# Query heads of the sliding attention transposed in pairs

## The chip, the cores and the metric
The kernel runs on one core of one Trainium2 chip. The metric is the device time of one execution in microseconds (us), lower is better. The engines are TensorE (PE for its matmuls, PEld for its weight loads), VectorE (DVE), ScalarE (ACT), GpSimd (POOL) and SyncE (SP), which issues the DMAs. Each works through its own queue of instructions in order; semaphores hold an instruction until what it needs is there.

## The reference
A decoder trunk of two layers on 1024 tokens of width 1024, float32. Three mixers read one normalised projection of 1312 columns; their outputs are concatenated, projected and added, and a gated feed-forward follows. The change touches the first mixer, sliding-window attention with 6 query heads on 2 key-value heads of 64, cut here to what matters:

```python
q = rms_norm(q.reshape(B, S, SWA_HEADS, HEAD_DIM), q_gain)
k = rms_norm(k.reshape(B, S, SWA_KV_HEADS, HEAD_DIM), k_gain)
s = jnp.einsum('bnqhgd,bnkhd->bnhgqk', qb, kb).astype(jnp.float32) * (HEAD_DIM ** -0.5)
s = jnp.where(mask[None, :, None, None], s + bias[None, None], -jnp.inf)
lse = jnp.logaddexp(jax.nn.logsumexp(s, axis=-1, keepdims=True), sk)
o = jnp.einsum('bnhgqk,bnkhd->bnqhgd', jnp.exp(s - lse).astype(v.dtype), vb)
```

Each block of 128 queries sees its own 128 keys and the 128 before.

## The kernel before
Each layer is three functions. `phase1` (from L283) goes over 8 tiles of 128 tokens: normalise and transpose the input tile (`head`, L330), project it in three pieces of 512, 512 and 288 columns (`proj`, L377, lines 381 to 383), and from these compute the sliding attention, the pooling mixer and the inputs of the latent attention. `phase2` (L545) is the latent attention with the output projection w_out (L787 to L817 and L795 to L797); `phase34` is the feed-forward.

Products are made of pieces: an operand is split into a high part, rounded to the type float32r by ACT, and a low part, the rest, by DVE (`split`, L57), and a product adds the piece products that matter. For the scores (L513, L514) the trick is in the contraction of 128: one operand holds the high part of a query head on partitions 0 to 63 and its low part on 64 to 127, and the key stands in both halves, so that one matmul adds both.

To get there, a tile's projected queries and keys `qk` (8 heads of 64: six of queries, two of keys) are multiplied by their norms into `dup`, in two rounds of four heads, each head written twice side by side (L401). Four PE transposes per round (L406) put 128 columns, one head in both halves, into one bank of PSUM, `tq`. ACT writes the scaled high part over all 128 partitions (L409), DVE overwrites the lower half with the low part (L410); the second round has two query heads and the two key heads, whose parts go to `kr5` by `split` (L414). `dup` is one buffer; `tq` shares a one-bank pool, `ps_ta`, with the transposes of L447 and L459 (in tile 7, `ps_th` with those of L339).

```python
tp = (ps_th if t >= 7 else ps_ta).tile([P, 4, P], F32, name="tq", tag="th" if t >= 7 else "ta")
sc.activation(dst, tp[:, 0:nq], AF.Copy, scale=gqc)
```

The program is written tile by tile; a scheduler sets the order on each engine across the tiles from its own estimates of durations, and pools decide what waits for a buffer. So an edit in one place can move instructions all over phase 1.

Of the kernel before, what the change touches and what calls it, by code (L numbers as in the profile page):

```python
# [11 lines left out]
F32 = mybir.dt.float32  # L12
# [3 lines left out]
AF = mybir.ActivationFunctionType  # L16
ALU = mybir.AluOpType
# [4 lines left out]
P = 128  # L22
# [14 lines left out]
def trunk(ctx: ExitStack, tc: tile.TileContext, A, out):  # L37
# [65 lines left out]
    for l in range(DEPTH):  # L103
        xsrc = A["x"][0] if l == 0 else xres
        G = dict(
            ident=ident, xm=xm, xrow=xrow, krr=krr, rc=rc, cosT=cosT, sinT=sinT, sinks=sinks,
            pscale=pscale, invc=invc, nhalf=nhalf, gq=gq, gm=gm, cmask=cmask, identr=identr, rn=rn, gc=gc, g32=g32, xsrc=xsrc, dram=dram, gap=gap, xp=xp, gns=ExitStack(), bias_keep=bias_keep)
        phase1(nc, tc, A, l, pool, split, f, bcast, G, (gq, gk, gmk, dram) if l == 0 else None)
        phase2(nc, tc, A, l, pool, split, f, bcast, G)
        phase34(nc, tc, A, l, pool, split, f, bcast, G, xres, out)  # L110


def rstd_of(nc, ms, n, nhalf):
    nc.gpsimd.tensor_scalar(out=ms, in0=ms, scalar1=EPS, scalar2=None, op0=ALU.add)
    nc.gpsimd.tensor_tensor(out=ms, in0=ms, in1=nhalf[:, 0:n], op=ALU.pow)
    return ms
# [16 lines left out]
def tables(nc, tc, load, A, bcast, early, one, evq, ps, kr5, G, more):  # L133
    ve, sc, gp, te, sy = nc.vector, nc.scalar, nc.gpsimd, nc.tensor, nc.sync
# [5 lines left out]
    sy.dma_start(rel[0:32], A["rel_bias"])  # L140
    hot = evq.tile([P, 512], F32, name="hot", tag="qk")[:, 0:384]
    sy.dma_start(hot[0:33], A["hot"])
    flip = evq.tile([P, 4, 128], F32, name="flip", tag="dup")
    sy.dma_start(flip[:, 0], A["flip"])
    acc = ps.tile([P, 512], F32, name="po")
    te.matmul(acc[0:6, 0:384], rel[0:33], hot[0:33], start=True, stop=True)
# [9 lines left out]
    for i in range(3):  # L156
        acc = ps.tile([P, 512], F32, name="po")
        c = slice(512 * i, 512 * i + 512)
# [65 lines left out]
    def cut(v, bits):  # L224
# [6 lines left out]
        out=ang, in0=posf.unsqueeze(2).to_broadcast(shp),  # L231
        in1=ifr.unsqueeze(1).to_broadcast(shp), op=ALU.mult,
# [33 lines left out]
    def wrap(v):  # L266
        up, dn = tmp(), tmp()
        ve.tensor_scalar(out=up, in0=v, scalar1=float(np.pi), scalar2=None, op0=ALU.is_gt)
        ve.tensor_scalar(out=dn, in0=v, scalar1=-float(np.pi), scalar2=None, op0=ALU.is_lt)
        fma(up, -TWO_PI, v, v)  # L270
        fma(dn, TWO_PI, v, v)
        ve.tensor_scalar(out=up, in0=v, scalar1=LIM, scalar2=-LIM, op0=ALU.min, op1=ALU.max)
        return up
# [5 lines left out]
    c = wrap(rs)  # L279
# [3 lines left out]
def phase1(nc, tc, A, l, pool, split, f, bcast, G, setup):  # L283
    ve, sc, gp, te, sy = nc.vector, nc.scalar, nc.gpsimd, nc.tensor, nc.sync
    cosT, sinT = G["cosT"], G["sinT"]
    ident, xm, xrow, krr = G["ident"], G["xm"], G["xrow"], G["krr"]
    with ExitStack() as ph:
# [9 lines left out]
        evq = pool(ph, f"p1q_{l}")  # L297
# [11 lines left out]
        ps_th = pool(ph, f"p1th_{l}", bufs=1, space=PSUM)  # L309
        ps_ta = pool(ph, f"p1ta_{l}", bufs=1, space=PSUM)  # L310
# [44 lines left out]
        kr5 = one.tile([P, 2, 2, 3 * P], F32R, name="kr5")  # L355
        if l == 0:
            tables(nc, tc, load, A, bcast, early, ev, evq, ps_o, kr5, G, setup)
# [3 lines left out]
        for g in range(4):  # L361
            o = 64 * (g % 2)
# [8 lines left out]
        for t in range(NT):  # L371
# [17 lines left out]
            qk = evq.tile([P, 512], F32, name="qk")  # L389
# [5 lines left out]
            r8 = rstd_of(nc, ms8, 8, G["nhalf"])  # L395
            qs = two.tile([P, 6, P], F32R, name="qs")
            gqc = G["gq"][:, l : l + 1]
            for b in range(2):
                dup = evq.tile([P, 4, 2, 64], F32, name="dup")
                sh = [P, 4, 2, 64]  # L400
                ve.tensor_tensor(  # L401
                    out=dup, in0=qk[:, 256 * b : 256 * b + 256].rearrange("p (h d) -> p h d", h=4).unsqueeze(2).to_broadcast(sh),
                    in1=r8[:, 4 * b : 4 * b + 4].unsqueeze(2).unsqueeze(3).to_broadcast(sh), op=ALU.mult)
                tp = (ps_th if t >= 7 else ps_ta).tile([P, 4, P], F32, name="tq", tag="th" if t >= 7 else "ta")
                for j in range(4):
                    te.transpose(tp[:, j], dup[:, j].rearrange("p a c -> p (a c)"), ident)  # L406
                nq = 4 if b == 0 else 2
                dst = qs[:, 4 * b : 4 * b + nq]
                sc.activation(dst, tp[:, 0:nq], AF.Copy, scale=gqc)  # L409
                ve.scalar_tensor_tensor(  # L410
                    out=dst[64:128], in0=tp[64:128, 0:nq], scalar=gqc[64:128], in1=f(dst[64:128]),
                    op0=ALU.mult, op1=ALU.subtract)
            kc = slice(slot * P, slot * P + P)
            split(kr5[:, 0, :, kc], kr5[:, 1, :, kc], tp[:, 2:4])  # L414
            if slot == 2:
                gp.tensor_copy(kr5[:, :, :, 0:P], f(kr5[:, :, :, 2 * P : 3 * P]))

# [28 lines left out]
            tp = ps_ta.tile([P, 4, P], F32, name="ta")  # L446
# [11 lines left out]
            tp = ps_ta.tile([P, 4, P], F32, name="ta")  # L458
# [4 lines left out]
            if t % 2 == 1:  # L463
                W = 16 + 2 * P
                for k in range(2):
# [4 lines left out]
                    if k == 1:  # L470
# [5 lines left out]
                                     in1=sa[64:128, st - hs : W - hs], op=ALU.add)  # L476
                    dd = one.tile([P, 2 * P], F32, name="dd")
                    for g, src in ((2 * k, sa), (2 * k + 1, sb)):
# [4 lines left out]
                            out=dd[pr], in0=src[pr, 16:W], scalar=wv, in1=u[pr, 16:W],  # L483
# [21 lines left out]
            for g in range(2):  # L505
# [3 lines left out]
                for i0, ni in ((0, 2), (2, 1)):  # L509
                    s = ps_sc.tile([P, 2, 256], F32, name="s")  # L510
                    for i in range(i0, i0 + ni):
                        h = 3 * g + i
# [4 lines left out]
                                     in1=G["bias"][:, h0 : h0 + ni, 256 - nk : 256], op=ALU.add)  # L517
                ve.tensor_reduce(mx[:, gs], Pt[:, :, 0 : nk + 1], AX.X, ALU.max, negate=True)
                for i in range(3):
                    h = 3 * g + i  # L520
# [3 lines left out]
                for i in range(3):  # L524
                    h = 3 * g + i
# [3 lines left out]
                for b in range(nb):  # L529
                    tp = ps_tp.tile([P, 4, P], F32, name="tp")  # L530
                    for i in range(3):
# [9 lines left out]
                                 in1=ob[0:64].rearrange("p (a b) -> p a b", a=3), op=ALU.add)  # L541
# [757 lines left out]
```

## Time and profile before

| | |
|---|---|
| three runs | 2209.97, 2216.93, 2217.36 us, median 2216.93 |
| profiled execution | 2210.4 us, its span 2208.6 us |
| granted TensorE clock, mean | 0.985 of full speed |
| PE busy | 2114.1 us, 96% |
| DVE busy | 1692.3 us, 77% |
| ACT busy | 1087.7 us, 49% |
| POOL busy | 976.2 us, 44% |

Phase 1 of layer 0 runs from the start to about 200 us, that of layer 1 from about 1109 to 1290 us; each overlaps the beginning of phase 2. The span begins at zero; a share of busy time is an average over the span, and a matmul's busy time runs from its start to a modelled end, while the next one may have started.

### The profile page before, as it was taken

The numbers are of one execution on the slowest core, as the hardware profiler recorded it, in microseconds if no ns is written. First come the engines' busy times: TensorE is split into PE (matmuls) and PEld (weight loads), VectorE is DVE, ScalarE is ACT, GpSimd is POOL, SyncE is SP. The second block draws the span as 40 slices with busy tenths as digits, with TensorE's granted clock in tenths as the row PEclk, the third lists the DMA queues.
The fourth block names the chain that finished last, engine by engine and source line by source line (L and its number), as shares of the span: only waits on it lengthen the run. The fifth ranks groups of instructions, "written<-read, shape, count | busy, mean of one in ns | idle before, by whom it ended". The sixth has DMA issues, their size and how long they took to land.

```text
span 2208.6 us, 29772 instructions
## 1 busy us (share of the span) xinstructions
PE 2114.1 (96%) x10468; PEld 1766.5 (80%) x10468; DVE 1692.3 (77%) x2595; ACT 1087.7 (49%) x2300; POOL 976.2 (44%) x916
## 2 busy tenths in 40 slices
PE   7998999999999999999989988999999999999999
PEld 5887788877788888788868867988778888887887
DVE  5567888898988787765845678887998888877657
ACT  5778767563434333311257786665634343343111
POOL 1433647245544452532614344462465444425215
PEclk8999999999999999999999999999999999999999
DMA  7002221323534435975530022113234443359754
GB/s 220 1 1 80 82 77 39 106 96 133 181 134 166 149 125 198 412 296 188 200 113 1 1 95 77 68 49 102 96 144 165 144 171 134 142 217 412 278 200 162
DMA packets 137932, 312.16 MB, mean 141 GB/s; under 512 B 17297, under 2 KB 68152, under 8 KB 137784
## 3 DMA queue, kind: packets, MB, share of 16 engines
q1 hardware_dynamic: 137784, 310.27, 39.4%
q8 instruction: 83, 1.36, 0.3%
q14 instruction: 65, 0.53, 0.1%
HBM read 203.53 MB, written 106.70 MB: 140 GB/s over the span
## 4 chain that ended last, share of the span: by engine, by line
PE 70%; DVE 10%; DMA 8%; ACT 6%; POOL 3%; issue 2%; SPq 1%; ACTq 0%; POOLq 0%; DVEq 0%
PE gu L1149 10%; PE gu L1147 10%; PE gu L1148 10%; PE dn L994 5%; PE dn L996 5%; PE dn L995 5%; PE acc L381 3%; PE acc L382 3%; PE acc L383 3%; DMA rw<-in_w_down_dram 2%; PE tp L756 2%; DMA raw<-in_w_in_dram 1%; PE ss L732 1%; PE po L766 1%; DMA raw<-in_w_gate_dram 1%
## 5 line engine op out<-in xcount | busy, mean ns | idle before, releaser
L1149 PE MATMUL gu<-T,sb 128*128 128x512 f32 x704 | 274.8, 391 | 9.8 <-DVE sb L58 9.7
L1147 PE MATMUL gu<-T,sb 128*128 128x512 f32 x704 | 274.9, 390 | 4.6 <-ACT sb L58 2.5
L1148 PE MATMUL gu<-T,sb 128*128 128x512 f32 x704 | 274.0, 389 | 0.0
L994 PE MATMUL dn<-op,ga 128*128 128x512 f32 x616 | 241.3, 393 | 7.4 <-DMA ga<-gd 7.4
L995 PE MATMUL dn<-op,ga 128*128 128x512 f32 x616 | 241.4, 392 | 0.0
L996 PE MATMUL dn<-op,ga 128*128 128x512 f32 x616 | 240.6, 392 | 0.0
L58 ACT CAST go<-xm 128x512 fp32r<-128x512 f32 x154 | 95.1, 620 | 274.4 <-POOL xm L1181 94.2
L943 POOL TENSOR_TENSOR rw<-rw 128x1536 f32<-128x1536 f32 (+1 forms) x32 | 112.4, 3522 | 257.0 <-DVE op L953 163.5
L1124 POOL TENSOR_TENSOR xm<-raw 128x512 f32<-128x512 f32 x44 | 68.6, 1561 | 319.9 <-DMA raw<-in_w_up_dram 122.8
L952 ACT CAST op<-rw 128x1536 fp32r<-128x1536 f32 (+1 forms) x56 | 76.9, 1376 | 266.7 <-PE dn L996 253.8
L58 DVE TENSOR_TENSOR go<-xm,go 128x512 fp32r<-128x512 f32 x154 | 154.4, 1012 | 34.1 <-ACT go L58 30.1
L58 ACT CAST sb<-raw 128x512 fp32r<-128x512 f32 x180 | 110.4, 617 | 122.5 <-PE gu L1149 99.6
L1149 PEld LDWEIGHTS gu<-T,sb 128*128 128x128 f32 x704 | 132.1, 188 | 41.3 <-DVE sb L58 13.9
L1147 PEld LDWEIGHTS gu<-T,sb 128*128 128x128 f32 x704 | 132.2, 188 | 34.5 <-ACT sb L58 4.6
L1181 POOL TENSOR_TENSOR xm<-xm 128x512 f32<-128x512 f32 x88 | 143.3, 1637 | 30.4 <-DVE go L58 19.6
L1148 PEld LDWEIGHTS gu<-T,sb 128*128 128x128 f32 x704 | 132.2, 188 | 27.4
L58 DVE TENSOR_TENSOR sb<-raw,sb 128x512 fp32r<-128x512 f32 x180 | 152.9, 850 | 1.0
L953 DVE TENSOR_TENSOR op<-rw,op 128x1536 fp32r<-128x1536 f32 (+1 forms) x56 | 113.8, 2032 | 40.0 <-ACT op L952 40.0
L994 PEld LDWEIGHTS dn<-op,ga 128*128 128x128 f32 x616 | 116.7, 189 | 33.3 <-issue 7.3
L1147 PE MATMUL gu<-B,A 128*128 128x512 f32 x336 | 132.1, 393 | 4.4 <-ACT B L58 4.4
L995 PEld LDWEIGHTS dn<-op,ga 128*128 128x128 f32 x616 | 116.7, 189 | 24.4
L996 PEld LDWEIGHTS dn<-op,ga 128*128 128x128 f32 x616 | 116.7, 189 | 24.3
(322 smaller groups left out, 6102.5 us busy)
## 6 DMA issues: line engine op xcount, KB each, us to landing
gd<-go SPq DMA_DIRECT2D x154, 512.0 KB, 3.1
ga<-gd SPq DMA_DIRECT2D x154, 512.0 KB, 5.7
raw<-in_w_gate_dram SPq DMA_DIRECT2D x22, 1024.0 KB, 5.6
raw<-in_w_up_dram SPq DMA_DIRECT2D x22, 1024.0 KB, 6.5
rw<-in_w_down_dram SPq DMA_DIRECT2D x44, 512.0 KB, 8.1
xp<-xt SPq DMA_DIRECT2D x32, 256.0 KB, 2.0
old<-xp SPq DMA_DIRECT2D x16, 512.0 KB, 4.1
xp<-xm SPq DMA_DIRECT2D x16, 512.0 KB, 2.9
```

What stands on the lines that cost most here:

```text
L58: return sc.copy(hi, src), ve.tensor_tensor(out=lo, in0=src, in1=f(hi), op=ALU.subtract)
L943: gp.tensor_tensor(out=o, in0=a, in1=b, op=ALU.subtract)
L952: sc.copy(t[:, 0], q[b])
L953: ve.tensor_tensor(out=t[:, 1], in0=q[b], in1=f(t[:, 0]), op=ALU.subtract)
L994: te.matmul(acc, S_[:, j, 0, ts], T_[:, 0, j], start=j == 0, stop=False)
L995: te.matmul(acc, S_[:, j, 0, ts], T_[:, 1, j], start=False, stop=False)
L996: te.matmul(acc, S_[:, j, 1, ts], T_[:, 0, j], start=False, stop=j == h - 1)
L1124: gp.tensor_tensor(out=s1, in0=q["A21"], in1=q["A22"], op=ALU.add)
L1147: te.matmul(acc, s[:, 0, k], b[:, 0, k], start=k == 0, stop=False)
L1148: te.matmul(acc, s[:, 0, k], b[:, 1, k], start=False, stop=False)
L1149: te.matmul(acc, s[:, 1, k], b[:, 0, k], start=False, stop=k == HK - 1)
L1181: gp.tensor_tensor(out=q[o], in0=q[a], in1=q[b], op=op)
```

## The change
Per tile the six query heads are multiplied by their norms once each, and the two key heads twice side by side, into one buffer of ten pieces of 64 (before: two rounds of eight). Two query heads make one 128-column transpose, three of these fill a first `tq`; the keys' two transposes fill a second. Even heads then lie on partitions 0 to 63, odd ones on 64 to 127. For each half ACT writes the high part in place and DVE writes the low part to the other half, both as 64 partitions x 3 heads x 128. An odd head so has its low part on top; the scores add the halves and are the same. In `tables` the buffer that shares `dup`'s place grows with it. From L424 on, line numbers of the changed kernel are 7 higher.

```diff
-            for b in range(2):
-                dup = evq.tile([P, 4, 2, 64], F32, name="dup")
-                sh = [P, 4, 2, 64]
+            dup = evq.tile([P, 10, 64], F32, name="dup")
+            for o, c, n, m in ((0, 0, 6, 1), (6, 6, 2, 2)):
+                sh = [P, n, m, 64]
                 ve.tensor_tensor(
-                    out=dup, in0=qk[:, 256 * b : 256 * b + 256].rearrange("p (h d) -> p h d", h=4).unsqueeze(2).to_broadcast(sh),
-                    in1=r8[:, 4 * b : 4 * b + 4].unsqueeze(2).unsqueeze(3).to_broadcast(sh), op=ALU.mult)
-                tp = (ps_th if t >= 7 else ps_ta).tile([P, 4, P], F32, name="tq", tag="th" if t >= 7 else "ta")
-                for j in range(4):
-                    te.transpose(tp[:, j], dup[:, j].rearrange("p a c -> p (a c)"), ident)
-                nq = 4 if b == 0 else 2
-                dst = qs[:, 4 * b : 4 * b + nq]
-                sc.activation(dst, tp[:, 0:nq], AF.Copy, scale=gqc)
+                    out=dup[:, o : o + n * m].rearrange("p (h m) d -> p h m d", m=m),
+                    in0=qk[:, 64 * c : 64 * (c + n)].rearrange("p (h d) -> p h d", h=n).unsqueeze(2).to_broadcast(sh),
+                    in1=r8[:, c : c + n].unsqueeze(2).unsqueeze(3).to_broadcast(sh), op=ALU.mult)
+            pair = dup.rearrange("p (j a) d -> p j (a d)", a=2)
+            wide = ps_th if t >= 7 else ps_ta
+            tp = wide.tile([P, 4, P], F32, name="tq", tag="th" if t >= 7 else "ta")
+            for j in range(3):
+                te.transpose(tp[:, j], pair[:, j], ident)
+            qv = qs.rearrange("p (j a) c -> p j a c", a=2)
+            for a in range(2):
+                top, low = slice(64 * a, 64 * a + 64), slice(64 - 64 * a, 128 - 64 * a)
+                sc.activation(qv[top, :, a], tp[top, 0:3], AF.Copy, scale=gqc[top])
                 ve.scalar_tensor_tensor(
-                    out=dst[64:128], in0=tp[64:128, 0:nq], scalar=gqc[64:128], in1=f(dst[64:128]),
+                    out=qv[low, :, a], in0=tp[top, 0:3], scalar=gqc[top], in1=f(qv[top, :, a]),
                     op0=ALU.mult, op1=ALU.subtract)
+            tp = wide.tile([P, 4, P], F32, name="tq", tag="th" if t >= 7 else "ta")
+            for j in range(2):
+                te.transpose(tp[:, j], pair[:, 3 + j], ident)
             kc = slice(slot * P, slot * P + P)
-            split(kr5[:, 0, :, kc], kr5[:, 1, :, kc], tp[:, 2:4])
+            split(kr5[:, 0, :, kc], kr5[:, 1, :, kc], tp[:, 0:2])
```

Phase 1's order changes on every engine; behind the first part of phase 2 it is the same in both. Two places follow, with what each row waits for in brackets (the engine named there is the one whose semaphore it waits for).

ACT in layer 0, the queries and keys of tile 1 (L409, and L58 on kr, of before; L413 and L58 on kr of the change), before:

```order
L409 ACTIVATE qs<-tq,gq 128x512 [waits PE_49]
L390 ACTIVATE qk<-acc,ms_942 128x512 [waits DVE_49,PE_49,Pool_49]
L333 ACTIVATE junk,ms_1467<-xm 128x1024 [waits DMAHW3_49]
L539 COPY ob<-po 64x384 [waits PE_49]
L392 ACTIVATE sq<-qk 128x512 [waits Activation_49]
L409 ACTIVATE qs<-tq,gq 128x256 [waits PE_49]
L58 CAST kr_325<-tq 128x2x128 [waits DVE_49]
```

and now:

```order
L413 ACTIVATE qs<-tq,gq 64x3x128 [waits PE_49]
L390 ACTIVATE qk<-acc,ms_934 128x512 [waits PE_49,Pool_49]
L333 ACTIVATE junk,ms_1451<-xm 128x1024 [waits DMAHW3_49]
L413 ACTIVATE qs<-tq,gq 64x3x128 [waits DVE_49]
L392 ACTIVATE sq<-qk 128x512 [waits Activation_49]
L546 COPY ob<-po 64x384 [waits PE_49]
L429 ACTIVATE vt<-acc,ms_934 128x2x64 [waits PE_49]
L58 CAST kr_325<-tq 128x2x128 [waits PE_49]
```

The second scaling waited for the second round's transposes on PE; it now waits for DVE's first subtract, and the keys' high part waits for PE alone.

PE in layer 1, tile 4, from the transposes of the keys (L406; now L419) to the first scores (L513; now L520). Before, it begins so:

```order
L406 MATMUL tq<-ident,dup 128x128 [waits DVE_49,PE_49]
L406 MATMUL tq<-ident,dup 128x128 x3
L383 MATMUL acc<-wb_10715,hT 128x512
L381 MATMUL acc<-wb_10716,hT 128x512
L382 MATMUL acc<-wb_10724,hT 128x512
L383 MATMUL acc<-wb_10716,hT 128x512
L339 MATMUL th<-ident,xm 128x128 [waits DVE_49]
L339 MATMUL th<-ident,xm 128x128 x3
L536 MATMUL po<-pT,vt 128x384 [waits Activation_49]
L381 MATMUL acc<-wb_10709,hT 128x288 [waits DVE_49,Activation_49]
```

with 23 more projection matmuls of 288 columns, one product and three transposes up to the first scores. Now, all that stands between the second transpose of the keys and the first scores, which are the last row:

```order
L381 MATMUL acc<-wb_10683,hT 128x288
L382 MATMUL acc<-wb_10691,hT 128x288
L383 MATMUL acc<-wb_10683,hT 128x288
L381 MATMUL acc<-wb_10684,hT 128x288
L382 MATMUL acc<-wb_10692,hT 128x288
L383 MATMUL acc<-wb_10684,hT 128x288
L500 MATMUL po<-dh,pwh 128x256 [waits PE_49,Activation_49]
L501 MATMUL po<-dl,pwh 128x256 [waits DVE_49]
L502 MATMUL po<-dh,pwl 128x256
L539 MATMUL tp<-ident,Pt 128x128 [waits DVE_49]
L539 MATMUL tp<-ident,Pt 128x128 x2
L520 MATMUL s<-kr_10805,qs 128x256 [waits Activation_49,Pool_49]
```

The keys' transposes moved down to six projection matmuls of 288 columns, three products and three transposes ahead of the scores. What stood between them and the scores stands ahead of them now, behind the transposes of the queries.

## Rows read from the trace of the kernel before

**Rows 1.** The page, busy us, share of the span and instructions by engine.

```profile
PE 2114.1 (96%) x10468; PEld 1766.5 (80%) x10468; DVE 1692.3 (77%) x2595; ACT 1087.7 (49%) x2300; POOL 976.2 (44%) x916
```

**Rows 2.** Busy time by stretch (counts in brackets), granted clock, DMA share, GB/s.

```profile
core 0: us, PE busy (x) PEld busy (x) DVE busy (x) ACT busy (x) POOL busy (x), PEclk, DMA share, GB/s
...
65.00:162.00 97.00, 96.90 (x557) 84.54 (x557) 55.74 (x107) 67.71 (x186) 38.21 (x89) 0.98 0.00 1
...
1126.00:1259.00 133.00, 131.66 (x760) 114.12 (x759) 74.18 (x145) 89.91 (x255) 46.25 (x104) 0.99 0.01 3
```

**Rows 3.** Timeline of PE at 65 us: start, us, what, idle before and releaser.

```profile
65.05 0.54 PE L536 MATMUL po<-pT,vt 128*128 128x384 f32 x1 [3.12 <-ACT pT L58]
```

**Rows 4.** Chain of waits, in order of time: start, us, what.

```profile
71.52 0.44 PE tq L406 x4
...
177.12 0.43 PE tq L406 x4
...
186.72 0.44 PE tq L406 x4
189.15 0.34 SPq L787
189.53 3.80 DMA raw<-in_w_out_dram
193.40 0.62 ACT wo L58
...
1267.05 0.44 PE tq L406 x4
...
1276.65 0.44 PE tq L406 x4
...
1279.42 4.50 DMA raw<-in_w_out_dram
```

**Rows 5.** Tile view of `tq`, PE, 65 to 162 and 1126 to 1259 us: min/median/max ns.

```profile
L406 PE MATMUL tq<-ident,dup x40: 270/272/273, 71.4 to 155.1; 128*128 128x128 f32 x40
L406 PE MATMUL tq<-ident,dup x48: 270/272/273, 1135.4 to 1249.8; 128*128 128x128 f32 x48
```

**Rows 6.** Timeline of PE around one group of four.

```profile
71.36 0.60 PE L406 MATMUL tq<-ident,dup 128*128 128x128 f32 x4
71.72 0.48 PE L382 MATMUL acc<-wa,hT 128*128 128x512 f32 x1
72.03 0.39 PE L383 MATMUL acc<-wa,hT 128*128 128x512 f32 x1
```

**Rows 7.** Views of `dup`, `kr`, L539 and L540: min/median/max ns, first and last start.

```profile
L401 DVE TENSOR_TENSOR dup<-qk,ms x32: 675/691/694, 33.2 to 1277.3; 128x512 f32<-128x512 f32 x32
L58 DVE TENSOR_TENSOR kr<-tq,kr x16: 412/424/426, 47.8 to 1288.0; 128x256 fp32r<-128x256 f32 x16
L539 ACT COPY ob<-po x32: 476/477/480, 67.7 to 1346.4; 64x384 f32<-64x384 f32 x32
L540 DVE TENSOR_TENSOR xm<-po,ob x32: 540/550/553, 68.3 to 1346.9; 64x384 f32<-64x384 f32 x32
```

**Rows 8.** Tile view of `qs`, ACT and DVE.

```profile
L409 ACT ACTIVATE qs<-tq,gq x32: 453/586/693, 41.1 to 1281.1; 128x512 fp32r<-128x512 f32 x16, 128x256 fp32r<-128x256 f32 x16
L410 DVE SCALAR_TENSOR_TENSOR qs<-tq,gq,qs x32: 490/624/758, 41.8 to 1283.3; 64x512 fp32r<-64x512 f32 x16, 64x256 fp32r<-64x256 f32 x16
```

**Rows 9.** Timeline of PE at the hand-over, layers 0 and 1.

```profile
197.40 0.55 PE L532 MATMUL tp<-ident,Pt 128*128 128x128 f32 x3 [1.98 <-DVE pT L58]
...
1288.16 0.90 PE L532 MATMUL tp<-ident,Pt 128*128 128x128 f32 x3 [2.16 <-DVE pT L58]
```

**Rows 10.** Waits, layer 0's hand-over: us in total, times, longest.

```profile
SPq L790 <- DVE wo L58: 1.7, 1, 1.7
...
DVE xt L816 <- PE po L797: 3.7, 3, 2.1
```

More of the change, by code (lines that the diff above doesn't have):

```diff
@@ L142, in tables @@
     sy.dma_start(hot[0:33], A["hot"])
-    flip = evq.tile([P, 4, 128], F32, name="flip", tag="dup")
+    flip = evq.tile([P, 5, 128], F32, name="flip", tag="dup")
     sy.dma_start(flip[:, 0], A["flip"])
```

## The prediction

> **What bounds the kernel now.** I read the page's busy shares first, then the busy table by stage, the chain of waits, the tile views of the tiles the change touches, and the timelines around them. The page says that TensorE (PE) is busy 96% and VectorE (DVE) 77% [rows 1]. An average over stages decides nothing here, so the table by stage comes next [rows 2]. The change touches phase 1 alone, which runs once per layer. From 65 to 162 us TensorE is busy 96.90 of 97.00 us and from 1126 to 1259 us 131.66 of 133.00, at a granted clock of 0.98 and 0.99; DVE is busy 55.74 and 74.18 us there, ScalarE (ACT) 67.71 and 89.91. These two stretches are bound by TensorE. Before 65 us it is not: the score-value product at 65.05 had waited 3.12 us for ACT [rows 3]. After phase 1 it is not either: at 189.53 and 1279.42 the chain of waits leaves TensorE for a load of w_out, 3.80 and 4.50 us, and stays with ACT for a while [rows 4].
>
> **The removed transposes.** Per tile of 128 tokens, eight PE transposes become five. The tile view gives 272 ns for each [rows 5], but that is a span from start to modelled end, and neighbours overlap. What one costs the queue is read from the chain and the timeline: a group of four stands on the chain with 0.44 us [rows 4], 0.11 each (0.44 / 4), and in the timeline the next projection matmul starts 0.36 us after the group's first [rows 6]. I take 0.11 us. Not all count. Layer 0's tile 0 lies before 65 us, under a chain of ACT and DMA: nothing. Tiles 1 to 5 of layer 0 (40 transposes) and 0 to 5 of layer 1 (48) lie in the bound stretches [rows 5]; tile 6 of both layers is on the chain as well, and of tile 7 the first group, just ahead of the w_out load [rows 4]; its second group falls under that load. The load itself is issued when the last weights of phase 1 are free, so it moves forward with TensorE. Counted: tiles 1 to 6 of layer 0 and 0 to 6 of layer 1, 13 tiles by three, and in each layer's tile 7 the one that its first group loses: 39 + 2 = 41. 41 x 0.11 = **4.5 us saved**. The bounds are nothing and, all 48 at their full 0.272, 13.1 us.
>
> By the Trainium skill, TensorE: Matmul & The Clock Gate, section Part 4: PE-mode transpose, a 128x128 transpose takes about 275 ns inside a kernel; 48 of them would be 13.2 us (an estimate from that page). The durations of rows 5 agree with that figure, the starts in rows 6 do not show it as a price.
>
> **DVE.** Two products of 128x512 (0.691 us each [rows 7]) become one of 384 and one of 256 columns. The nearest rows are 0.550 us for 64x384 and 0.424 for 128x256 [rows 7]: 0.97 instead of 1.38, 0.41 saved per tile, 6.6 us in all. DVE has room of over 40 us in each bound stretch [rows 2], so I count nothing; TensorE's queue covers it, and the bound below nothing is nothing, since DVE work only falls.
>
> **The four halves.** ACT scaled 128x512 and 128x256 (0.693 and 0.453), DVE subtracted 64x512 and 64x256 (0.758 and 0.490) [rows 8]. Now each runs twice on 64 partitions x 384 columns. Half way between the rows that is 0.573 and 0.624: the same sum, 1.15 and 1.25 us, so nothing. Other 64x384 rows on these engines are 0.477 and 0.550 [rows 7], so it could be 0.2 and 0.15 less per tile, also under TensorE. The DVE now writes to the other partition half than it reads. L540 does the same for one of its two groups and in place for the other, and its 32 durations lie between 540 and 553 ns [rows 7]: no price for crossing.
>
> **The new wait.** In the new order ACT's second scaling waits for DVE's first subtract, every time. From the first group's transposes to a free PSUM bank, before: 0.69 + 0.76 = 1.45 us; now 0.573 + 0.624 + 0.573 + 0.624 = 2.39 us, 0.95 more, in which the keys' transposes wait, and behind the waiting scaling stand ACT's copies for other tiles. In exchange the second bank holds only keys: of the queries' 0.453 and 0.490 us that stood between it and the key split [rows 8] nothing is left. So scores start about as long after the first transposes as before, and meanwhile projection matmuls stand in TensorE's queue, as the excerpts of the order show. I take nothing. The bounds: 0.5 us per tile won (nothing, under TensorE) and 0.95 lost.
>
> **Order and addresses.** The scheduler rearranges all of phase 1, and hardly anything behind it. On SP one load of w_out (L790) moves ahead of one load of x (L811) in each layer. It waited 1.7 us in SP's queue for DVE [rows 10], so that load of x, and the loads and stores behind it, can come up to that much later; the sums on that x (L816) wait for TensorE's product, 2.1 us at the longest [rows 10], which covers it. The larger buffer moves later tiles of phase 1 by 512 bytes; the layer's weight loads keep their places. Both at nothing, with the hand-over to phase 2 open by about the waits it has now: TensorE stands 1.98 and 2.16 us in one wait there [rows 9], so plus or minus 2 us a layer.
>
> **Sum.** 2210.4 us (span 2208.6 and 1.8 around it) - 4.5 = 2205.9. The median of the runs shown is 2216.93; of the four executions two lie near 2210 and two near 2217, 7 us apart, mean 2213.7. For a median that can fall in either group I forecast 2213.7 - 4.5 = **2209 us**; its own range is 2204 to 2214.
>
> **The rivals.**
> *A transpose costs its whole duration.* If it neither overlaps its neighbours nor lets them start, 48 x 0.272 = 13.1 us go: 2200.6. The durations speak for it [rows 5]; the pitch of 0.11 in rows 4 and 6 against. 13%. [...]
> *Given back at the hand-over.* ACT, POOL and DVE work through their own chain behind the w_out load [rows 4]; if that chain does not move forward, or if the new order spreads it worse by 2 us a layer [rows 9], the 4.5 are gone: 2213.7, no change. Against it: the load is released by TensorE's last projection. 17%.
> *The longer serial chain shows (slower).* The place is the keys' transposes and the first scores of each tile: ACT, DVE, ACT, DVE in turn, each in its queue behind other work. If none of the 0.95 us is covered, 16 x 0.95 = 15.2 us come on top of the 48 x 0.11 = 5.3 saved: + 9.9, or 2223.6. It decides from about 0.3 us of new waiting per tile (4.5 / 16). For it: the new order puts fewer matmuls between the keys' transposes and the scores. Against it: TensorE's waits in the stretches now add up to 0.1 and 1.34 us [rows 2], so the present order covers chains of this length well. 15%.
>
> **How the numbers follow.** The forecast has the remaining 55%. A measurement of this kernel can tell some 0.5% from no change, 11 us: below 2205.8 counts as faster than the median shown, above 2228 as slower. Faster: nearly all of the first rival and the fifth of the forecast that ends in the lower group of runs, 0.12 + 0.11 = 0.23. Slower: the upper third of the last rival and a scheduling accident, 0.06. The rest, 0.71, is no change. The range reaches from the first rival with a little over (2199) to the last with a little under (2222).
>
> **What would show it.** Right: the bound stretch of layer 0 is shorter by 5 x 0.33 = 1.6 us and that of layer 1 by 6 x 0.33 = 2.0 us, and TensorE's busy share stays above 98%; transposes still stand 0.11 us apart; DVE's busy time falls by about 7 us, ACT's stays; the 64x384 operations last 0.48 to 0.62 us; everything behind the hand-over keeps its length. Wrong: TensorE waiting for ACT's second scaling or for the key split in many tiles; a hand-over that is longer by 4 us or more; phase 1 shorter by 6 us a layer.

## The result, and the profile after

The changed kernel takes 2199.38 us (median of 6 runs, 2197.11 to 2207.41), the kernel before in the same comparison 2213.11 (6 runs): a ratio of 0.9945, 95% interval 0.9922 to 0.9968, so 12 us or 0.55% faster (the two medians lie 13.7 apart; over all executions the means are 12.0 apart, see the table below). Forecast were 2209 us and a gain of 4.5. The sign held, and the range (2199 to 2222) by 0.4 us, but some 7.5 of the 12 us were not in the sum.

The profiled execution took 2197.31 us (span 2195.5), 13.1 less than that of before. The page's busy line, against [rows 1]:

```profile
PE 2104.7 (96%) x10420; PEld 1757.7 (80%) x10420; DVE 1697.9 (77%) x2595; ACT 1089.6 (50%) x2300; POOL 974.3 (44%) x916
```

TensorE has 48 instructions fewer. Now the busy table of the two stretches in the middle of phase 1, with the columns of [rows 2]:

```profile
65.00:162.00 97.00, 95.14 (x542) 82.29 (x543) 55.48 (x110) 73.80 (x205) 36.71 (x91) 1.00 0.00 1
...
1126.00:1259.00 133.00, 131.96 (x769) 115.67 (x770) 76.53 (x155) 96.60 (x267) 50.37 (x117) 1.00 0.02 6
```

TensorE still bounds them, with 98% and 99% busy. Then the tile view of `tq` and `qs` (duration ns min/median/max, first and last start), which answers to [rows 5, 8]:

```profile
L409 PE MATMUL tq<-ident,dup x48: 270/272/273, 35.7 to 1272.2; 128*128 128x128 f32 x48
...
L413 ACT ACTIVATE qs<-tq,gq x32: 561/576/582, 40.8 to 1279.1; 64x384 fp32r<-64x384 f32 x32
L414 DVE SCALAR_TENSOR_TENSOR qs<-tq,gq,qs x32: 609/616/625, 41.4 to 1279.9; 64x384 fp32r<-64x384 f32 x32
...
L419 PE MATMUL tq<-ident,dup x32: 270/272/328, 43.5 to 1280.7; 128*128 128x128 f32 x32
```

Last TensorE's timeline around one group of three, against [rows 6]:

```profile
72.02 0.40 PE L383 MATMUL acc<-wa,hT 128*128 128x512 f32 x1
72.26 0.49 PE L409 MATMUL tq<-ident,dup 128*128 128x128 f32 x3
72.50 0.48 PE L381 MATMUL acc<-wa,hT 128*128 128x512 f32 x1
```

Each transpose still shows 272 ns, and three of them hold back the next matmul by 0.24 us.

**Where the time went, by layer.** I cut each layer in three: to the start of phase 1's last projection matmul, to that of phase 2's last output product into `ss`, and the feed-forward part, to its last down product. These marks are the last start in the line's own view. Here are those of layer 0 and then of layer 1, of before and below it of after:

```profile
L383 PE MATMUL acc<-wb,hT x128: 290/388/628, 33.3 to 188.8; 128*128 128x512 f32 x64, 128*128 128x288 f32 x64
...
L795 PE MATMUL ss<-wot,ch x12: 387/396/496, 430.9 to 450.4; 128*128 128x512 f32 x12
...
L383 PE MATMUL acc<-wb,hT x102: 290/300/481, 1149.9 to 1278.8; 128*128 128x288 f32 x54, 128*128 128x512 f32 x48
...
L795 PE MATMUL ss<-wot,ch x12: 387/396/501, 1531.7 to 1551.2; 128*128 128x512 f32 x12
```

```profile
L383 PE MATMUL acc<-wb,hT x128: 290/344/476, 32.6 to 186.2; 128*128 128x512 f32 x64, 128*128 128x288 f32 x64
...
L802 PE MATMUL ss<-wot,ch x12: 389/397/526, 434.9 to 454.4; 128*128 128x512 f32 x12
...
L383 PE MATMUL acc<-wb,hT x101: 290/301/481, 1150.1 to 1271.3; 128*128 128x288 f32 x53, 128*128 128x512 f32 x48
...
L802 PE MATMUL ss<-wot,ch x12: 389/398/497, 1519.5 to 1539.0; 128*128 128x512 f32 x12
```

In us, before and after: layer 0, 188.8 / 261.6 / 653.6 and 186.2 / 268.2 / 651.3; layer 1, 174.8 / 272.4 / 652.3 and 165.6 / 267.7 / 651.4. So phases 1 and 2 together became 4.0 us longer in layer 0 and 13.9 us shorter in layer 1, though both lose the same 24 transposes. Removed work alone cannot look like that.

**Three shares of a stage.** From the busy table in stretches of 4 us I take TensorE's idle time (length less busy time), its loss at a low granted clock (busy time x (1 - granted clock)), and what is left, the work at full clock. The time in phases 1 and 2 of both layers is the sum of the three. Each row is one profiled execution, whose own time stands in the fourth column; the mean is over all executions of the kernel, of before those that ran beside the experiments (73, and two more, of 4199 and 7442 us, left out).

| kernel | transposes a tile | mean us | profiled us | phases 1 + 2 | idle | low clock | work |
|---|---|---|---|---|---|---|---|
| before | 8 | 2213.1 | 2210.4 | 897.6 | 63.7 | 20.7 | 813.2 |
| before, second profile | 8 | | 2213.8 | 901.6 | 63.8 | 22.6 | 815.2 |
| after | 5 | 2201.1 | 2197.3 | 887.7 | 61.7 | 16.5 | 809.5 |
| after, second profile | 5 | | 2203.3 | 891.1 | 59.1 | 20.6 | 811.4 |
| after, 3 idle transposes | 8 | 2207.9 | 2199.2 | 888.8 | 61.0 | 15.1 | 812.7 |
| after, 8 idle transposes | 13 | 2222.6 | 2227.4 | 914.8 | 66.0 | 24.4 | 824.4 |
| before, rounds exchanged | 8 | 2209.5 | 2204.4 | 896.1 | 58.6 | 20.6 | 817.0 |
| before, one wide `dup` | 8 | 2210.6 | 2209.1 | 897.4 | 61.7 | 20.9 | 814.8 |
| before, keys apart | 8 | 2215.5 | 2214.6 | 903.3 | 66.9 | 26.0 | 810.6 |
| after, scalings first | 5 | 2215.6 | 2213.7 | 905.9 | 69.0 | 27.9 | 809.0 |
| after, keys apart | 5 | 2197.0 | 2195.8 | 884.6 | 59.9 | 16.0 | 808.7 |
| after, keys apart, second profile | 5 | | 2199.1 | 885.0 | 58.3 | 17.9 | 808.8 |
| after, keys apart and first | 5 | 2212.1 | 2206.2 | 894.9 | 65.3 | 19.0 | 810.5 |

The work column has an error of some 2 us (two executions of one kernel differ by as much), the low clock one of up to 4, and a mean over executions one of 1 to 2. A profiled execution can lie far from its kernel's mean, 8.7 us below it with three idle transposes.

### The profile page after: what moved, and what is told of

Read it like the earlier page. It is cut to its first block, busy times and chain, and to the rows that moved or that the text cites. A ratio compares the mean times of both kernels' runs of the same rounds, so it can differ in the third digit from the quotient of the medians.

```text
span 2195.5 us, 29665 instructions
## 1 busy us (share of the span) xinstructions
PE 2104.7 (96%) x10420; PEld 1757.7 (80%) x10420; DVE 1697.9 (77%) x2595; ACT 1089.6 (50%) x2300; POOL 974.3 (44%) x916
## 4 chain that ended last, share of the span: by engine, by line
PE 71%; DVE 11%; DMA 8%; ACT 5%; issue 2%; POOL 2%; SPq 1%; DVEq 0%; ACTq 0%; POOLq 0%
PE gu L1156 10%; PE gu L1154 10%; PE gu L1155 10%; PE dn L1001 5%; PE dn L1003 5%; PE dn L1002 5%; PE acc L381 3%; PE acc L382 3%; PE acc L383 3%; DMA rw<-in_w_down_dram 2%; PE tp L763 2%; PE po L804 1%; PE po L802 1%; DMA ga<-gd 1%; PE po L803 1%
## 5 line engine op out<-in xcount | busy, mean ns | idle before, releaser
L58 ACT CAST go<-xm 128x512 fp32r<-128x512 f32 x154 | 94.9, 620 | 292.3 <-POOL xm L1188 103.0
L959 ACT CAST op<-rw 128x1536 fp32r<-128x1536 f32 (+1 forms) x56 | 76.8, 1376 | 261.6 <-PE dn L1003 250.6
L58 DVE TENSOR_TENSOR go<-xm,go 128x512 fp32r<-128x512 f32 x154 | 157.5, 1033 | 41.1 <-ACT go L58 37.0
L58 ACT CAST sb<-raw 128x512 fp32r<-128x512 f32 x180 | 110.3, 616 | 115.3 <-PE gu L1156 92.2
L58 DVE TENSOR_TENSOR sb<-raw,sb 128x512 fp32r<-128x512 f32 x180 | 154.0, 856 | 0.9
```

Of the source, the lines that this page charges most:

```text
L58: return sc.copy(hi, src), ve.tensor_tensor(out=lo, in0=src, in1=f(hi), op=ALU.subtract)
L959: sc.copy(t[:, 0], q[b])
```

## The experiments

Theory A: the gain is the transposes, at the 0.11 us by which they hold back their successor. Rival C: the transposes, at their whole 272 ns; 2200.6 us, which is where the time came out. Theory B: A's 4 to 5 us, and the rest because the scheduler, given another text, places phase 1 and the hand-over otherwise, so that TensorE waits less and keeps its clock more.

**1. Each kernel again.** No edit.

> The changed kernel, unaltered, for a second profile and a narrower interval. All theories: 0.990 to 0.998 of the kernel before. If the gain behind the 4.5 us of transposes is a matter of the single execution (which short waits of TensorE are followed by a lower granted clock), the stages of this profile differ from those of the first profile of this kernel by 3 us or more in phase 2 and in the feed-forward stages, whose instructions are the same; if the gain is fixed by the new order, phase 1 is again about 186 us in layer 0 and 166 us in layer 1 (188.8 and 174.8 before the change) and each later stage agrees with the first profile within 2 us.

Measured: 0.9949 (0.9937 to 0.9962). Phase 1 is 184.9 and 166.2 us, as in the first profile; the later stages are 1.2 to 2.4 us longer than there (269.9, 652.6, 270.1 and 652.6 us), the largest of them between the two expectations. So phase 1's length belongs to the order; what differs between two executions is mostly the clock (27.8 us lost in all against 21.4), of which more below.

> The kernel before, unaltered, for a second profile. If the 174.8 us of phase 1 in layer 1 belong to its order, they come again within 3 us, with a wait of some 2 us for ScalarE's weights (wb) near 1125 us and two of some 2 us at the hand-over near 1285 us; the 9 us by which the change is shorter there are then its own. If they belong to the single execution, phase 1 of layer 1 is 171 us or less.

Measured: 2213.78 us. Phase 1 of layer 1 is 173.4 us. TensorE waits again for `wb`, 1.74 and 1.68 us, and at the hand-over 1.07 and 3.10 us. So its length in layer 1 is the order's own, in both kernels.

**2. Doses of transposes.** Idle transposes are put into the changed kernel, into columns of PSUM that nobody reads; three per tile:

```diff
+            te.transpose(tp[:, 3], pair[:, 0], ident)
...
-            for j in range(2):
-                te.transpose(tp[:, j], pair[:, 3 + j], ident)
+            for j in range(4):
+                te.transpose(tp[:, j], pair[:, 3 + j % 2], ident)
```

> The changed kernel with three idle transposes of 128x128 per tile put back, into columns of PSUM that nobody reads: eight transposes per tile again, the rest of the change untouched. Theory A (a transpose costs TensorE its pitch of 0.11 us): 48 x 0.11 = 5.3 us over the changed kernel, some 2204.7, ratio 0.996 to 0.997 to the kernel before. Rival C (a transpose costs its whole 0.272 us): 13.1 us over, some 2212.5, ratio 1.000. Theory B (the transposes are worth little, the new order and the shorter waits gave the gain): within 2 us of the changed kernel, ratio 0.9945 to 0.995.

Measured: 0.9976 (0.9959 to 0.9993), mean 2207.9, 6.8 us over the changed kernel. A's size, with an error of 2; half of C's 13.1. But a dose changes the order as well: in TensorE's timelines from 40 to 190 us, 583 of the changed kernel's 795 matmuls other than these transposes stand in the same sequence in this kernel, against 790 in the second profile of the unaltered one. So a mean time alone does not price a transpose. Its one profile shows 2.3 us of it as work (812.7 against 810.4 in the mean of the changed kernel's two), within that column's error, so a larger dose was needed.

Eight per tile: four more in the first group and four in the second.

```diff
+            for j in range(4):
+                te.transpose(tp[:, 3], pair[:, j % 3], ident)
...
-            for j in range(2):
-                te.transpose(tp[:, j], pair[:, 3 + j], ident)
+            for j in range(6):
+                te.transpose(tp[:, j if j < 2 else 3], pair[:, 3 + j % 2], ident)
```

> The changed kernel with eight idle transposes of 128x128 more per tile, thirteen in all, into PSUM columns that nobody reads: a second, larger dose. Theory A at the pitch of 0.11 us: 128 x 0.11 = 14.1 us over the changed kernel's mean of 2201.1, some 2215, ratio 1.001. By the price that three per tile showed (6.8 us for 48, or 5.9 at equal clock): 16 to 18 us, 2217 to 2219, ratio 1.002 to 1.003. Rival C, 0.272 us each: 35 us, 2236, ratio 1.010. Theory B (their number matters little, order and waits do): under 2207.

Measured: 1.0036 (1.0020 to 1.0052), mean 2222.6, 21.5 us over the changed kernel. Not C's 35, and not B's 6 at the most. The profiled execution, with 2227.42 us above the mean, has 14.0 us more work than the mean of the changed kernel's two (824.4 against 809.5 and 811.4), which is A's 14.1; the other 11 us of that execution are idle time and low clock (90.4 against 78.2 and 79.7). The timeline of TensorE in this kernel shows the price directly:

```profile
83.70 0.82 PE L421 MATMUL tq<-ident,dup 128*128 128x128 f32 x6
84.28 0.38 PE L381 MATMUL acc<-wb,hT 128*128 128x288 f32 x1
```

Six transposes hold back the next matmul by 0.58 us, 0.10 each, while each is recorded with 272 ns. By the Trainium skill, TensorE: Matmul & The Clock Gate, section Part 4: PE-mode transpose, a 128x128 transpose (bf16) took about 275 ns in a kernel; the trace agrees for its duration, and the work column and this timeline show that it is not what a transpose costs a full queue. C falls.

**3. The same work in another order.** The kernel before, with its two rounds exchanged:

```diff
-            for b in range(2):
+            for b in (1, 0):
...
-            kc = slice(slot * P, slot * P + P)
-            split(kr5[:, 0, :, kc], kr5[:, 1, :, kc], tp[:, 2:4])
+                kc = slice(slot * P, slot * P + P)
+                if b == 1:
+                    split(kr5[:, 0, :, kc], kr5[:, 1, :, kc], tp[:, 2:4])
```

> The kernel before with the two rounds of a tile exchanged: the round with the keys first, its split before the other round. Every instruction of the kernel before is there, eight transposes per tile, in another order. Theory B (a good part of the gain comes from how the scheduler places phase 1, whatever is removed): the time moves by 4 us or more, ratio 0.998 or below, or 1.002 or above, and the stages that move are phase 1 of layer 1 and the hand-over behind it. Theories A and C (the removed work alone): 0.999 to 1.001, phase 1 as long as before within 2 us.

Measured: 0.9986 (0.9973 to 0.9999), mean 2209.5, 3.6 us less than before: in the mean more than A and C allow and short of B's 4, and the interval reaches into both. Phase 1 of layer 1 did not get shorter (176.3 us). Other stages moved, both ways: phase 1 of layer 0 is 4.4 us shorter than in the first profile of before (184.4), phase 2 there 8.2 longer (269.8), phase 2 of layer 1 6.8 shorter (265.6), with nothing removed. The time by itself does not decide.

**4. One part of the change alone: the joined buffer.**

```diff
-    flip = evq.tile([P, 4, 128], F32, name="flip", tag="dup")
+    flip = evq.tile([P, 8, 128], F32, name="flip", tag="dup")
...
+            dups = evq.tile([P, 8, 2, 64], F32, name="dup")
             for b in range(2):
-                dup = evq.tile([P, 4, 2, 64], F32, name="dup")
+                dup = dups[:, 4 * b : 4 * b + 4]
```

> The kernel before with one buffer of twice the width for the doubled queries of both rounds, so that the second product need not wait for a buffer whose transposes of the first round are still to come; that is the part of the change that joins the two buffers, alone, with all eight transposes, four full scalings and four full subtracts per tile. Theory B (waits and order): 0.996 to 0.998, some 5 to 8 us faster, most of it in phase 1 of layer 1. Theories A and C (removed transposes alone): 1.000 within 0.001.

Measured: 0.9986 (0.9975 to 0.9998), mean 2210.6, 2.5 us less: between the two expectations, with an interval that reaches into both. The buffer is 8 pieces of 128 columns wide here and 5 in the change, so the addresses behind it differ too. Phase 1 of layer 1 is 4.1 us shorter than before (170.7).

**5. The changed kernel without its alternating wait.** Both scalings are written ahead of both subtracts:

```diff
             for a in range(2):
-                top, low = slice(64 * a, 64 * a + 64), slice(64 - 64 * a, 128 - 64 * a)
+                top = slice(64 * a, 64 * a + 64)
                 sc.activation(qv[top, :, a], tp[top, 0:3], AF.Copy, scale=gqc[top])
+            for a in range(2):
+                top, low = slice(64 * a, 64 * a + 64), slice(64 - 64 * a, 128 - 64 * a)
                 ve.scalar_tensor_tensor(
```

> The changed kernel with both scalings on ScalarE written ahead of both subtracts on VectorE, so that the second scaling no longer waits for the first subtract. The forecast put that new wait at nothing: then the time stays within 2 us of the changed kernel, ratio 0.994 to 0.9955 to the kernel before. The rival (the longer serial chain is paid in part): at 0.25 us or more a tile, 4 us or more faster than the changed kernel, ratio 0.993 or below.

Measured: 1.0007 (0.9992 to 1.0022), mean 2215.6: 14.5 us slower than the changed kernel, outside both expectations. The tile view of this kernel shows the same operations with the same durations:

```profile
L413 ACT ACTIVATE qs<-tq,gq x32: 560/576/581, 40.2 to 1283.1; 64x384 fp32r<-64x384 f32 x32
L416 DVE SCALAR_TENSOR_TENSOR qs<-tq,gq,qs x32: 610/616/626, 41.4 to 1284.4; 64x384 fp32r<-64x384 f32 x32
```

What grew are TensorE's waits (its timeline in layer 1, late phase 1 and hand-over; idle before, and releaser, in brackets):

```profile
1262.32 0.41 PE L421 MATMUL tq<-ident,dup 128*128 128x128 f32 x2 [2.12 <-DVE qs L416]
...
1288.44 0.55 PE L541 MATMUL tp<-ident,Pt 128*128 128x128 f32 x3 [2.91 <-DVE pT L58]
1289.93 0.50 PE L804 MATMUL po<-wo,mh 128*128 128x512 f32 x1 [0.41 <-ACT wo L58]
1291.29 0.69 PE L545 MATMUL po<-pT,vt 128*128 128x384 f32 x1 [0.85 <-ACT pT L58]
```

Idle and low clock in phases 1 and 2 are 96.9 us, 17 to 19 more than in the changed kernel, the work is the same 809. A text that only puts one of two independent steps first eats the whole gain of the change.

**6. Tile 7's keys in the other PSUM bank.** The changed kernel's timeline at layer 1's hand-over; layer 1's wait of [rows 9] is gone, and another stands in its place, 4.58 us for the queries' second subtract, which empties the bank:

```profile
1280.55 0.44 PE L419 MATMUL tq<-ident,dup 128*128 128x128 f32 x2 [4.58 <-DVE qs L414]
...
1283.24 0.80 PE L802 MATMUL po<-wo,mh 128*128 128x512 f32 x1 [0.56 <-DVE kr L58]
```

```diff
-            tp = wide.tile([P, 4, P], F32, name="tq", tag="th" if t >= 7 else "ta")
+            tp = ps_ta.tile([P, 4, P], F32, name="tq", tag="ta")
             for j in range(2):
```

> The changed kernel with the keys' transposes of tile 7 in the other PSUM bank, so that they need not wait until the queries have been read out of the first. In both profiles of the changed kernel TensorE waits 4.58 and 3.92 us in layer 1 for that (the subtract L414), with a granted clock below 1 behind it that cost 2.9 us. If that is the price of the longer serial chain, this kernel is 4 to 7 us faster than the changed one, ratio 0.9915 to 0.993 to the kernel before, and the keys' transposes of tile 7 wait for nothing. If the same wait turns up a few instructions later (in the score products that need these keys, or in the products of phase 2), the time stays within 2 us: ratio 0.994 to 0.9955.

> The changed kernel with the keys apart, unaltered, for more executions and a second profile: ratio 0.989 to 0.993 to the kernel before if the gain of 5 us over the changed kernel is its own, 0.994 or more if it was a matter of the executions.

Measured: 0.9908 (0.9889 to 0.9928) and 0.9935 (0.9915 to 0.9955); over the twelve executions the mean is 2197.0, 4.1 us less than the changed kernel (error 1.4), the fastest kernel here; the second ratio alone falls between the two expectations of it. And the reason is not the one that was expected:

```profile
1274.20 0.44 PE L419 MATMUL tq<-ident,dup 128*128 128x128 f32 x2 [1.49 <-ACT uT L469]
1276.39 0.79 PE L802 MATMUL po<-wo,mh 128*128 128x512 f32 x1 [1.75 <-DVE qs L414]
```

In layer 1 the wait shrank and turned up again at the next product, and phases 1 and 2 are as long there as in the changed kernel (434.5 and 435.2 us against 433.3 and 436.3). The gain stands in layer 0: 450.0 and 449.8 against 454.4 and 454.8. There the changed kernel has this wait (2.21 us in its second profile), which is in neither profile of the kernel with the keys apart; why the edit removes it stays open:

```profile
233.23 0.80 PE L804 MATMUL po<-wo,mh 128*128 128x512 f32 x1 [2.22 <-DVE mh L58]
```

The same step in the kernel before:

```diff
-                tp = (ps_th if t >= 7 else ps_ta).tile([P, 4, P], F32, name="tq", tag="th" if t >= 7 else "ta")
+                tp = (ps_th if (t, b) == (7, 0) else ps_ta).tile([P, 4, P], F32, name="tq", tag="th" if (t, b) == (7, 0) else "ta")
```

> The kernel before with the key round of tile 7 in the other PSUM bank, the step that made the changed kernel 5 us faster, without the change itself: eight transposes per tile, as many operations on every engine as before. If the one bank at the last tile costs the kernel before as much (its waits at the hand-over are 1.98 and 2.16 us there), 3 to 6 us faster, ratio 0.997 to 0.9985. If it became a cost only with the change's longer serial chain, 1.000 within 0.001.

Measured: 1.0015 (1.0005 to 1.0026), mean 2215.5, 2.4 us slower. It takes a constraint away and loses; among TensorE's waits is a new one in layer 0:

```profile
234.54 0.80 PE L797 MATMUL po<-wo,mh 128*128 128x512 f32 x1 [4.26 <-DVE mh L58]
```

**7. Keys apart, and written first.** The two transposes of the keys and their split ahead of the queries' three.

```diff
+            tp = ps_ta.tile([P, 4, P], F32, name="tq", tag="ta")
+            for j in range(2):
+                te.transpose(tp[:, j], pair[:, 3 + j], ident)
...
+            split(kr5[:, 0, :, kc], kr5[:, 1, :, kc], tp[:, 0:2])
             wide = ps_th if t >= 7 else ps_ta
...
-            tp = ps_ta.tile([P, 4, P], F32, name="tq", tag="ta")
-            for j in range(2):
-                te.transpose(tp[:, j], pair[:, 3 + j], ident)
...
-            split(kr5[:, 0, :, kc], kr5[:, 1, :, kc], tp[:, 0:2])
```

> The kernel with the keys apart, and the keys' two transposes and their split written ahead of the queries' three transposes: the same instructions in another order, five transposes per tile. If the removed work is what counts (theory A), it stays within 2 us of the kernel with the keys apart (mean 2195.8), ratio 0.990 to 0.993. If the order sets waits worth several us (theory B), it differs from it by 4 us or more, either way, and TensorE's idle time and low clock in the first two phases differ by as much, while the work there stays at 809 to 811 us in the two layers together.

Measured: 0.9999 (0.9988 to 1.0010), mean 2212.1, 15 us slower than with the keys second, and no faster than before, with three transposes a tile fewer. Its work is 810.5 us, its idle time and low clock 84.3 against 75.9 and 76.2. These 8 us belong to the profiled executions, which lie 8.8 apart (2206.2 against 2195.8 and 2199.1); the rest of the 15 is in no profile. Of its waits at layer 1's hand-over the longest are these:

```profile
1283.62 0.55 PE L539 MATMUL tp<-ident,Pt 128*128 128x128 f32 x3 [1.02 <-DVE pT L58]
1285.54 0.50 PE L802 MATMUL po<-wo,mh 128*128 128x512 f32 x1 [1.38 <-ACT wo L58]
...
1293.32 0.44 PE L543 MATMUL po<-pT,vt 128*128 128x384 f32 x1 [1.21 <-ACT pT L58]
...
1326.77 0.50 PE L804 MATMUL po<-wo,mh 128*128 128x512 f32 x1 [2.52 <-DVE mh L58]
```

**What follows.** Four kernels issue the changed kernel's operations, in different orders and partly with other PSUM buffers: 2197.0, 2201.1, 2212.1 and 2215.6, 18.6 us apart, mean 2206.5. Four issue those of the kernel before: 2209.5, 2210.6, 2213.1 and 2215.5, mean 2212.2. The two groups overlap, so the 5.7 us between their means have an error nearly as large. The work column is what shows A: it differs by 4.3 (means of six profiles each, 813.9 with eight and 809.7 with five), with an error of 1. Of the 12.0 us between before and after, some 4 are that work; 6.4 more are the idle time and low clock of the one order that this text happened to get (85.4 before and 79.0 after, means of two profiles), about half of each; the rest is within the error or behind phase 2.

So B holds in this form: the same operations, placed otherwise, move the time by more than the removed ones are worth. What in the placement does it stays open. Every edit moved many instructions at once, a kernel that keeps the order fixed while one moves was not tried, and the order was not parted from the addresses and banks that move with it; the durations of the operations that the change touches came out as forecast.

## Why the prediction was right and wrong

- *TensorE bounds phase 1*: right, 98% busy in the stretch of layer 0 and 99% in that of layer 1 (131.96 of 133.00).
- *0.11 us for a transpose, 4.5 us in all*: right in size. The pitch is 0.08 to 0.10 us in the timelines, the work fell by 4.3 us, and eight more per tile added 14.0 us of work.
- *The rival of the whole duration*: it gave 2200.6 us, next to the result, and is wrong. A time that fits does not show a mechanism; the doses did. The lower end of the range, 2199, was taken from this rival, so that the result of 2199.38 lies inside it is luck.
- *DVE*: the products fell from 22.0 us (32 of 688 ns) to 16.0 in the view by line:

```profile
L401 DVE TENSOR_TENSOR dup<-qk,ms 128x384 f32<-128x384 f32 x16 | 9.3, 580 | 6.4 <-PE tq L419 5.0 <-POOL ms L115 1.1
L401 DVE TENSOR_TENSOR dup<-qk,ms 128x256 f32<-128x256 f32 x16 | 6.7, 418 | 0.0
```

  That is 6.0 saved of the 6.6 forecast, off the path. DVE's whole busy time did not fall, though: 1692.3 before, 1697.9 after. Untouched operations took longer, most of all in the feed-forward part, and the second profile of before has 1697.3, so a sum of that size cannot be read from one execution.
- *The halves at 0.573 and 0.624 us, no price for crossing to the other partitions*: 0.576 and 0.616.
- *The new wait at nothing*: it is in the profile (DVE is idle 13.9 us for ACT's scalings, in 13 places, before 5.9 in 7; ACT 2.3 us for the subtract), and TensorE itself is idle for the subtract, 4.58 us at layer 1's hand-over. The bound of 0.5 us won has no row behind it; it entered no sum. Whether the wait costs could not be parted from the order, since the kernel without it is slower for other waits.
- **The step that failed** is *order and addresses: both at nothing, the hand-over plus or minus 2 us a layer*. It measured +3 us in layer 0 and -13 in layer 1 (means of two profiles each, phases 1 and 2), of which 4 us are the removed work. With it, *everything behind the hand-over keeps its length* fell: phase 2 of layer 0 grew by 7 us, 2 of them matmuls that moved behind phase 1's last projection, and 4 lower clock. Two of the forecast's own signs of being wrong showed, each in one layer: this one, and phase 1 of layer 1, 9 us shorter. What the rival *given back at the hand-over* expected, the gain lost again, is what layer 0 shows; layer 1 shows the opposite.
- *The base of 2213.7 from two groups of runs* was right: 2213.1 over 73 executions.

The trace of before could not give the order's value, but it could have given a wider bound: idle time and low clock in phases 1 and 2 are 84 us there, and no row said how much of that another order can move; the bound of 4 us (2 a layer) was only argued. The four orders of the changed kernel's work lie up to 9 us on either side of their mean.

## What to carry to other kernels

Where a scheduler rearranges a stage after any edit, the edit's own work and the new order are two terms, and the second can be the larger: here some 4 us against 18 between the best and the worst order. Run two or three neutral rewrites of the same work before an edit is called good, and keep the best order apart from the edit's credit. Price an operation on a full queue by how far it pushes its successor, not by its recorded duration, and prove that with a dose whose work is read apart from the order that it changes.

## What was not expected of the hardware

Whether the granted clock falls at a place is not fixed by the program. Here is phase 2 in layer 1 in the first and in the second execution of the changed kernel, where the same instructions come 1.7 us later in the second (columns of [rows 2], the clock is the third number from the end):

```profile
1456.00:1460.00 4.00, 2.55 (x13) 1.86 (x13) 2.27 (x8) 3.98 (x12) 1.56 (x2) 1.00 0.42 131
1460.00:1464.00 4.00, 4.00 (x26) 3.56 (x26) 3.04 (x5) 1.86 (x5) 4.00 (x3) 1.00 0.01 4
1464.00:1468.00 4.00, 4.00 (x29) 3.61 (x28) 3.35 (x6) 2.54 (x5) 3.02 (x2) 1.00 0.00 0
```

```profile
1456.00:1460.00 4.00, 2.72 (x20) 2.06 (x19) 3.90 (x9) 3.15 (x10) 2.07 (x2) 1.00 0.30 110
1460.00:1464.00 4.00, 3.61 (x15) 3.14 (x16) 1.38 (x5) 2.09 (x7) 2.86 (x2) 0.59 0.20 70
1464.00:1468.00 4.00, 4.00 (x15) 3.48 (x15) 2.21 (x2) 1.10 (x2) 1.81 (x2) 0.56 0.00 0
```

In both, TensorE is busy for 2.55 and 2.72 of the first 4 us. Its longer waits there, in the first execution and then in the second:

```profile
1457.78 0.39 PE L773 MATMUL po<-pT,vT 128*128 128x256 f32 x1 [0.34 <-DVE pT L58]
...
1459.22 0.30 PE L763 MATMUL tp<-ident,Pt 128*128 128x128 f32 x1 [0.82 <-ACT Pt L749]
```

```profile
1459.83 0.39 PE L773 MATMUL po<-pT,vT 128*128 128x256 f32 x1 [0.92 <-DVE pT L58]
...
1460.85 0.45 PE L763 MATMUL tp<-ident,Pt 128*128 128x128 f32 x1 [0.39 <-DVE sm L751]
```

They stand before the same two instructions and are about as long together (1.16 and 1.31 us), though not each. In one execution TensorE goes on at a granted clock of 1.00, in the other at 0.59 and 0.56, near the lower of its two levels, 1.2 GHz; the loss is 3.61 x 0.41 + 4.00 x 0.44 = 3.2 us. In the two profiles each of before and after, read in stretches of 4 us, a drop costs 1.3 to 4.6 us, most of them under 1.8 or near 3. By the Trainium skill, TensorE: Matmul & The Clock Gate, section A second HAM failure mode: psum-queue depth-cycling, short idle times between groups of matmuls can make the clock alternate; these rows agree, and show that one program's executions part there. The spread of a kernel's times goes with it: the twelve executions with three idle transposes run from 2199.24 us at a mean granted clock of 0.989 to 2217.92 at 0.982.
